# Half SwiGLUs with three pairs of places for split weights, splits queued one weight ahead, and normed operands after the third column block

## The chip, the cores and the metric

One core of a Trainium2 chip runs the whole program in one launch. The metric is device time in microseconds, the median of several executions. The profile is one more execution, recorded by the hardware profiler; its span goes from the first to the last instruction of the program. Engines: TensorE (PE for matmuls, PEld for its weight loads), VectorE (DVE), ScalarE (ACT), GpSimd (POOL) and SyncE (SP), which here only issues DMAs.

## What is computed

One step of a two-layer diffusion backbone on 128 context and 256 latent tokens, model width 1024, all in float32. Every sub-layer is an RMSNorm with a shift and a scale from the condition (adaLN), a mixer, and a gated residual. The two layers are

```
even: half SwiGLU -> gated DeltaNet | windowed attention -> half SwiGLU
odd : half SwiGLU -> bidirectional gated linear attention -> half SwiGLU
```

and the four half SwiGLUs, which the change is about, are each

```
h = rmsnorm(x) * (1 + scale) + shift
x = x + 0.5 * gate * ((silu(h @ Wg) * (h @ Wu)) @ Wd)      # Wg, Wu: 1024 x 2816, Wd: 2816 x 1024
```

Context and latent tokens have their own shift, scale and gate: nine vectors of 1024 a layer (18 in all, two streams each), each of them `silu(cond) @ ada_w + ada_b`.

## The kernel before

**Layout.** Activations lie transposed: 128 channels on the partitions, 8 blocks (`KD`) of channels, 384 tokens (`T`) in the free dimension. To keep float32 accuracy every matmul is done three times: weights and activations are split in a high and a low part in the `F32R` format, and `products` (L189) issues low x high, high x low and high x high for every block of 128 input channels.

**Splitting a weight.** `split_w` takes a 128 x 1024 tile `w` from a ring of three places, loads it with a DMA on SyncE's queue (L174), copies it on ScalarE to `wh` (L176) and lets VectorE subtract, `wl = w - wh` (L177). `wh` and `wl` come from a ring of two places each. A place comes free when the products that read it are done.

**A half SwiGLU** (`ffn`, called four times, f = 0 to 3) goes through four stages. In the first gate and up stage, called h1 below, it makes 11 column blocks j of 128: a product with the gate weight (24 matmuls), one with the up weight (24 more), `scaled` (L203: VectorE multiplies the PSUM result by `rb`, the reciprocal norm of each token), silu on ScalarE (L332), the multiplication (L337), and a split of the result into `ah` and `al` (L181, L182). In the first down stage, a1, eight output blocks m are made of two weights each, of 768 and 640 columns (18 and 15 matmuls, 33 an m), and added to x (`residual`, L305, two instructions, one per token stream). Then the same for the other 11 column blocks (h2) and the rest of the down projection (a2). In a2 the next norm is prepared behind each m: `norm_tile` (L247, L249) scales x to `hh` and `hl`, `square_tile` sums squares, and after the last m `end_norm` makes `rb` by way of two small matmuls (L289, L297) and a copy (L300).

**The norm is applied late.** `hh` and `hl` hold x times the scale, without the norm. The shift stands as two more columns (`TC` = 386), so that the product with the shift falls out of the same matmul and is added as a bias behind `scaled`.

**adaLN steps.** While a half SwiGLU runs, VectorE also works out later adaLN vectors: `ada_rows` loads 128 x 1024 tiles of `ada_w` (`aw`, two places, a DMA on SyncE's queue, L103), and multiplies each for both streams into accumulators (L145 for the first tile, L147 for the seven others). One such instruction is one step, 16 steps a vector; then `ada_sum` sums over partitions with 16 small matmuls (L161) and `ada_end` stores the vector. f = 0 makes five vectors, f = 1 and f = 2 four each, f = 3 one. The steps are put in by the local function `between`: two or three after each j, two after each m of a1, one after each m of a2, queued behind that block's last VectorE instruction. The order of the engines' queues is otherwise the compiler's: it places instructions in program order, and takes a later one first where the earlier has to wait in its own model.

**Early weights.** Behind the last column blocks of f = 0 and f = 2, `side` splits five weights of the mixer that follows into places the mixer uses later (`Even.weights`, `Odd.weights`).

## Time and profile before

| | |
|---|---|
| median of 3 runs | 1725.99 us (1721.74 to 1726.15) |
| the profiled execution | 1724.06 us; span 1722.3 us |
| PE busy | 1656.9 us, 96% of the span |
| DVE / ACT / POOL busy | 72% / 44% / 0% |
| mean granted TensorE clock | 0.985 |

The profile's page counts a pipelined matmul as busy from its start to a modelled end, and two matmuls overlap. A busy PE is therefore not yet a PE that could go no faster; what shows its pace is how many matmuls a stretch holds. DMA issues are not counted as busy.

### The profile page before, as it was taken

How to read it: one execution, taken by the hardware profiler on the slowest of the kernel's cores; microseconds unless marked ns; L12 is line 12 of the kernel's file. 1: busy time of each engine (PE TensorE's matmuls, PEld its weight loads, DVE VectorE, ACT ScalarE, POOL GpSimd, SP SyncE). 2: the span in 40 equal slices, each digit the busy share in tenths (PEclk: the TensorE clock that was granted, in tenths of full speed). 3: DMA queues.
4: the chain of work that ended last, by engine and by line, in shares of the span. 5: the costliest groups of instructions: out<-in, count | busy, mean ns of one | idle time of the engine just before them, and what ended most of it. 6: DMA issues, size and time to landing. Idle time of an engine off the chain costs nothing.

```text
span 1722.3 us, 26237 instructions
## 1 busy us (share of the span) xinstructions
PE 1656.9 (96%) x10341; PEld 1570.9 (91%) x10341; DVE 1237.5 (72%) x2091; ACT 749.2 (44%) x1301; POOL 0.2 (0%) x4
## 2 busy tenths in 40 slices
PE   5999998999999999999999999999999999999997
PEld 3998998899888899989999998999898889999997
DVE  3887787777868768877856887786567768744554
ACT  4432343366336443323344432344655754433343
POOL 0000000000000000000000000000000000000000
PEclk8999999999999989999999999999999999999998
DMA  8566666451321226666644656574313354434332
GB/s 321 183 186 186 204 205 210 148 188 62 114 78 50 77 84 196 180 198 196 185 132 147 197 187 198 188 228 135 102 62 96 102 172 147 159 111 136 126 110 95
DMA packets 80376, 261.83 MB, mean 152 GB/s; under 512 B 9691, under 2 KB 11739, under 8 KB 80124
## 3 DMA queue, kind: packets, MB, share of 16 engines
q1 hardware_dynamic: 80252, 260.15, 47.8%
q8 instruction: 81, 1.33, 0.3%
q14 instruction: 43, 0.35, 0.1%
HBM read 255.13 MB, written 4.98 MB: 151 GB/s over the span
## 4 chain that ended last, share of the span: by engine, by line
PE 82%; DVE 10%; DMA 4%; issue 2%; ACT 2%; SPq 0%; DVEq 0%; ACTq 0%
PE acc L189 71%; DVE acc L147 3%; DVE wl L177 2%; DMA aw<-in_adaw_dram 2%; PE ada L161 1%; DVE x L305 1%; DMA w<-in_evw_dram 1%; DMA w<-in_wdn_dram 1%; PE ps L679 1%; PE ps L683 1%; PE ada L113 1%; PE ss L289 1%; PE ps L1139 1%; PE ps L647 0%; DVE ssum L276 0%
## 5 line engine op out<-in xcount | busy, mean ns | idle before, releaser
L176 ACT CAST wh<-w 128x1024 fp32r<-128x1024 f32 (+1 forms) x358 | 340.2, 951 | 683.5 <-PE acc L189 491.0
L189 PE MATMUL acc<-hh,wl 128*128 128x386 f32 x1728 | 595.3, 345 | 7.3 <-DVE wl L177 7.2
L189 PE MATMUL acc<-hl,wh 128*128 128x386 f32 x1728 | 589.6, 341 | 0.0
L189 PE MATMUL acc<-hh,wh 128*128 128x386 f32 x1728 | 587.9, 340 | 0.0
L177 DVE TENSOR_TENSOR wl<-w,wh 128x1024 fp32r<-128x1024 f32 (+1 forms) x358 | 392.3, 1097 | 98.3 <-ACT wh L176 96.8
L189 PEld LDWEIGHTS acc<-hh,wl 128*128 128x128 f32 x1728 | 325.6, 188 | 19.4 <-DVE wl L177 9.5
L189 PEld LDWEIGHTS acc<-hl,wh 128*128 128x128 f32 x1728 | 327.2, 189 | 2.3 <-issue 0.8
L189 PEld LDWEIGHTS acc<-hh,wh 128*128 128x128 f32 x1728 | 325.5, 188 | 2.3 <-issue 0.8
L189 PE MATMUL acc<-ah,wl 128*128 128x384 f32 x704 | 242.2, 344 | 17.2 <-DVE wl L177 16.8
L147 DVE SCALAR_TENSOR_TENSOR acc<-aw,cs,acc 128x1024 f32<-128x1024 f32 x196 | 243.1, 1278 | 8.4 <-DMA aw<-in_adaw_dram 8.4
L189 PE MATMUL acc<-al,wh 128*128 128x384 f32 x704 | 238.5, 339 | 0.0
L189 PE MATMUL acc<-ah,wh 128*128 128x384 f32 x704 | 238.4, 339 | 0.0
L189 PEld LDWEIGHTS acc<-ah,wl 128*128 128x128 f32 x704 | 132.7, 189 | 27.9 <-DVE wl L177 27.9
L189 PEld LDWEIGHTS acc<-al,wh 128*128 128x128 f32 x704 | 132.9, 189 | 0.0
L189 PEld LDWEIGHTS acc<-ah,wh 128*128 128x128 f32 x704 | 132.8, 189 | 0.0
L203 DVE TENSOR_TENSOR tu<-acc,rb 128x386 f32<-128x386 f32 x88 | 49.2, 559 | 105.7 <-PE acc L189 105.6
L203 DVE TENSOR_TENSOR tg<-acc,rb 128x386 f32<-128x386 f32 x138 | 76.6, 555 | 55.3 <-PE acc L189 52.0
L305 DVE SCALAR_TENSOR_TENSOR x<-acc,hg,x 128x128 f32<-128x128 f32 (+1 forms) x128 | 47.5, 413 | 68.5 <-PE acc L189 68.5
L332 ACT ACTIVATE sg<-tg 128x128 f32<-128x128 f32 (+1 forms) x176 | 70.6, 448 | 51.6 <-DVE tg L203 51.5
L337 DVE SCALAR_TENSOR_TENSOR a<-tu,sg 128x128 f32<-128x128 f32 (+1 forms) x176 | 65.7, 415 | 8.3
L181 ACT CAST ah<-a 128x384 fp32r<-128x384 f32 x88 | 45.3, 515 | 41.5 <-DVE a L337 41.3
L182 DVE TENSOR_TENSOR al<-a,ah 128x384 fp32r<-128x384 f32 x88 | 48.6, 552 | 3.5 <-ACT ah L181 3.5
(368 smaller groups left out, 1502.4 us busy)
## 6 DMA issues: line engine op xcount, KB each, us to landing
w<-in_wgu_dram SPq DMA_DIRECT2D x176, 512.0 KB, 3.7
aw<-in_adaw_dram SPq DMA_DIRECT2D x144, 512.0 KB, 4.2
w<-in_wdn_dram SPq DMA_DIRECT2D x64, 384.0 KB, 3.1
w<-in_wdn_dram SPq DMA_DIRECT2D x64, 320.0 KB, 3.0
w<-in_evw_dram SPq DMA_DIRECT2D x24, 512.0 KB, 4.1
w<-in_odw_dram SPq DMA_DIRECT2D x24, 512.0 KB, 3.6
w<-in_evo_dram SPq DMA_DIRECT2D x8, 512.0 KB, 3.5
w<-in_odo_dram SPq DMA_DIRECT2D x8, 512.0 KB, 4.0
```

Of the source, the lines that this page charges most:

```text
L113: nc.tensor.matmul(ps[32 * g:32 * g + 32, 0:256], self.cs[:, k, :], w[:, 256 * g:256 * g + 256], start=k == 0, stop=k == KD - 1)
L147: nc.vector.scalar_tensor_tensor(t, w, cs, t, op0=ALU.mult, op1=ALU.add)
L161: self.nc.tensor.matmul(ps[32 * g:32 * g + 32, 0:256], self.pick[:, s], acc[s][:, 256 * g:256 * g + 256], start=s == 0, stop=s == 1)
L176: nc.scalar.copy(wh[:, 0:n], w[:, 0:n])
L177: nc.vector.tensor_tensor(wl[:, 0:n], w[:, 0:n], wh[:, 0:n].bitcast(F32), op=ALU.subtract)
L181: self.nc.scalar.copy(hi, src)
L182: return self.nc.vector.tensor_tensor(lo, src, hi.bitcast(F32), op=ALU.subtract)
L189: self.nc.tensor.matmul(out, s[:, sl], mv[:, k0 + k], start=first and k == 0 and i == 0, stop=last and k == nk - 1 and i == 2)
L203: self.nc.vector.tensor_tensor(t[0:m], p, self.rb[0:m], op=ALU.mult)
L305: i = nc.vector.scalar_tensor_tensor(self.x[:, k, lo:hi], p[:, lo:hi], gate[:, k, s:s + 1], self.x[:, k, lo:hi], op0=ALU.mult, op1=ALU.add)
L332: nc.scalar.activation(sg[:, lo:hi], tg[:, lo:hi], AF.Silu, bias=tg[:, T + s:T + s + 1])
L337: nc.vector.scalar_tensor_tensor(a32[:, lo:hi], tu[:, lo:hi], tu[:, T + s:T + s + 1], sg[:, lo:hi], op0=ALU.add, op1=ALU.mult)
```

## The change

1. `split_w` takes every third pair of weight places of a half SwiGLU from the pool of that half SwiGLU, so that three pairs rotate in place of two.
2. `ffn` lists its 76 weights in the order of use, and `weights(n)` splits the next one before it hands out the present one: in program order every split stands one weight ahead.
3. `between` goes. `n` steps for each weight fall due behind the split, queued behind its VectorE instruction (`issue_after(self.last_split.ins)`): 2.8 a column block in f = 0 and 2.4 in the others, none in the first three; one a weight in a1, half a one in a2.
4. The DMAs of `ada_rows` are issued on GpSimd's queue, and every third `aw` tile has a place of its own, three in all.
5. From the fourth column block on (`raw = 3`), the products read `nh` and `nl`: x with norm, scale and shift applied, split once. `normed` makes them, eight blocks k over the first three j. These products have 384 columns, silu reads PSUM and is one instruction, and `scaled` and the two multiplications become one multiplication from PSUM.
6. Three weights instead of five are split early for each mixer, and three places (`XT`, `BR`, `mhl`) move to the mixer's own pool. The late steps also sum a vector one step pair earlier.

```diff
@@ -98,9 +99,9 @@
-    def ada_tile(self, v, k, pool=None):
+    def ada_tile(self, v, k, pool=None, queue=None):
         w = (pool or self.adar).tile([128, 1024], F32, tag="aw", name=self.name("aw"))
-        self.nc.sync.dma_start(w, self.a["adaw"][v // 2, k, v % 2])
+        (queue or self.nc.sync).dma_start(w, self.a["adaw"][v // 2, k, v % 2])
         return w
@@ -136,16 +137,16 @@
         for v in vs:
-            acc = [pool.tile([128, 1024], F32, tag=f"acc{s}", bufs=2, name=self.name("acc")) for s in range(2)]
+            acc = [pool.tile([128, 1024], F32, tag="acc", bufs=4, name=self.name("acc")) for s in range(2)]
             for k in range(KD):
-                w = self.ada_tile(v, k)
+                w = self.ada_tile(v, k, pool if k % 3 == 2 else None, nc.gpsimd)
                 for s in range(2):
                     t, cs = acc[s], self.cs[:, k, s:s + 1]
                     if k == 0:
                         nc.vector.tensor_scalar(t, w, cs, None, op0=ALU.mult)
                     else:
                         nc.vector.scalar_tensor_tensor(t, w, cs, t, op0=ALU.mult, op1=ALU.add)
-                    if k == 1 and s == 1 and ready:
+                    if k == 0 and s == 1 and ready:
                         self.ada_sum(*ready)
@@ -170,16 +171,20 @@
         nc = self.nc
+        if self.third and not to:
+            self.turn += 1
+            if self.turn % 3 == 0:
+                to = [self.third.tile([128, 1024], F32R, tag=t, name=self.name(t)) for t in ("wh", "wl")]
         w = self.ring.tile([128, 1024], F32, tag="w", bufs=3, name=self.name("w"))
         nc.sync.dma_start(w[:, 0:n], src)
         wh, wl = to or [self.ring.tile([128, 1024], F32R, tag=t, bufs=2, name=self.name(t)) for t in ("wh", "wl")]
         nc.scalar.copy(wh[:, 0:n], w[:, 0:n])
-        nc.vector.tensor_tensor(wl[:, 0:n], w[:, 0:n], wh[:, 0:n].bitcast(F32), op=ALU.subtract)
+        self.last_split = nc.vector.tensor_tensor(wl[:, 0:n], w[:, 0:n], wh[:, 0:n].bitcast(F32), op=ALU.subtract)
         return wh, wl
-    def split(self, hi, lo, src):
+    def split(self, hi, lo, src, engine=None):
         self.nc.scalar.copy(hi, src)
-        return self.nc.vector.tensor_tensor(lo, src, hi.bitcast(F32), op=ALU.subtract)
+        return (engine or self.nc.vector).tensor_tensor(lo, src, hi.bitcast(F32), op=ALU.subtract)
@@ -189,12 +194,13 @@
-    def proj(self, src, m=128):
+    def proj(self, src, m=128, h=None):
         w = src if isinstance(src, tuple) else self.split_w(src, KD * m)
         p = self.acc.tile([128, 512], F32, tag="acc", name=self.name("acc"))
-        self.products(p[0:m, 0:TC], w, self.hh, self.hl, KD, m, True, True)
-        return p[0:m, 0:TC]
+        n = TC if h is None else T
+        self.products(p[0:m, 0:n], w, *(h or (self.hh, self.hl)), KD, m, True, True)
+        return p[0:m, 0:n]
@@ -307,39 +313,73 @@
         return i
-    def ffn(self, f, l, gate, after, rows=(), side=iter(()), skip=0):
+    def ffn(self, f, l, gate, after, rows=(), side=iter(()), skip=0, steps=2):
         nc = self.nc
+        gs, shift = self.gs, self.m(l, gate - 2)
         hg = self.small.tile([128, KD, 2], F32, tag="hg", name=self.name("hg"))
         with self.tc.tile_pool(name=self.name("ffn"), bufs=1) as pool:
             ah = pool.tile([128, NF // 2, T], F32R, name=self.name("ah"))
             al = pool.tile([128, NF // 2, T], F32R, name=self.name("al"))
-            work = lambda tag, n: pool.tile([128, n], F32, tag=tag, bufs=2, name=self.name(tag))
+            h = [pool.tile([128, KD, T], F32R, name=self.name(t)) for t in ("nh", "nl")]
             rows = self.ada_rows(rows, pool) if rows else iter(())
-            def between(last, n):
-                with self.tc.issue_after(last.ins):
-                    for _ in range(n):
-                        next(rows, None)
+            self.third = pool
+            raw, due = 3, 0.0
+            wgu, wdn = self.a["wgu"], self.a["wdn"]
+            srcs = []
+            for half in range(2):
+                srcs += [(wgu[f, i], 1024) for i in range(NF * half, NF * half + NF)]
+                srcs += [(wdn[f, half, m, :, c0:c1], (c1 - c0) * 128) for m in range(KD) for c0, c1 in ((0, 6), (6, 11))]
+            srcs.reverse()
+            ready = [self.split_w(*srcs.pop())]
+            def weights(n):
+                nonlocal due
+                if srcs:
+                    ready.append(self.split_w(*srcs.pop()))
+                    due += n
+                    with self.tc.issue_after(self.last_split.ins):
+                        while due >= 1:
+                            next(rows, None)
+                            due -= 1
+                return ready.pop(0)
+            def normed(k):
+                t = self.tmp.tile([128, T], F32, tag="xg", name=self.name("nx"))
+                nc.vector.tensor_tensor(t, self.x[:, k], self.rb[:, 0:T], op=ALU.mult)
+                for s, lo, hi in STREAMS:
+                    nc.scalar.activation(t[:, lo:hi], t[:, lo:hi], AF.Identity, bias=shift[:, k, s:s + 1],
+                                         scale=gs[:, k, s:s + 1])
+                self.split(h[0][:, k], h[1][:, k], t)
             for half in range(2):
                 for jj in range(NF // 2):
                     j = half * (NF // 2) + jj
-                    pg = self.proj(self.a["wgu"][f, 2 * j])
-                    tg = self.scaled(pg)
-                    sg = work("sg", T)
-                    for s, lo, hi in STREAMS:
-                        nc.scalar.activation(sg[:, lo:hi], tg[:, lo:hi], AF.Silu, bias=tg[:, T + s:T + s + 1])
-                    pu = self.proj(self.a["wgu"][f, 2 * j + 1])
-                    tu = self.scaled(pu, work("tu", TC))
-                    a32 = work("a32", T)
-                    for s, lo, hi in STREAMS:
-                        nc.vector.scalar_tensor_tensor(a32[:, lo:hi], tu[:, lo:hi], tu[:, T + s:T + s + 1],
-                                                       sg[:, lo:hi], op0=ALU.add, op1=ALU.mult)
-                    last = self.split(ah[:, jj], al[:, jj], a32)
+                    hj, n = (None, 0.0) if j < raw else (h, steps / 2)
+                    pg = self.proj(weights(n), h=hj)
+                    a = pool.tile([128, T], F32, tag="a", bufs=3, name=self.name("a"))
+                    if j < raw:
+                        tg = self.scaled(pg)
+                        for s, lo, hi in STREAMS:
+                            nc.scalar.activation(a[:, lo:hi], tg[:, lo:hi], AF.Silu, bias=tg[:, T + s:T + s + 1])
+                        for k in range(KD * j // raw, KD * (j + 1) // raw):
+                            normed(k)
+                    else:
+                        nc.scalar.activation(a, pg, AF.Silu)
+                    pu = self.proj(weights(n), h=hj)
+                    if j < raw:
+                        tu = self.scaled(pu)
+                        for s, lo, hi in STREAMS:
+                            nc.vector.scalar_tensor_tensor(a[:, lo:hi], tu[:, lo:hi], tu[:, T + s:T + s + 1],
+                                                           a[:, lo:hi], op0=ALU.add, op1=ALU.mult)
+                    else:
+                        nc.vector.tensor_tensor(a, pu, a, op=ALU.mult)
+                    self.split(ah[:, jj], al[:, jj], a)
                     if j >= skip:
                         next(side, None)
-                    between(last, 2 + j % 2)
                 if half == 0:
                     nc.vector.tensor_scalar(hg, self.m(l, gate), 0.5, None, op0=ALU.mult)
                 else:
@@ -347,15 +387,14 @@
                     for c0, c1 in ((0, 6), (6, 11)):
-                        w = self.split_w(self.a["wdn"][f, half, m, :, c0:c1], (c1 - c0) * 128)
-                        self.products(p[:, 0:T], w, ah, al, c1 - c0, 128, c0 == 0, c1 == 11, k0=c0)
-                    last = self.residual(p, m, hg)
-                    between(last, 2 - half)
+                        self.products(p[:, 0:T], weights(1.0 - half / 2), ah, al, c1 - c0, 128, c0 == 0, c1 == 11, k0=c0)
+                    self.residual(p, m, hg)
                     if half == 1:
                         next(side, None)
                         after(m)
             for _ in rows:
                 pass
+            self.third = None
@@ -385,7 +424,7 @@
         self.early = {}
-        for j, tag, bufs in ((0, "LA", 6), (1, "LA", 6), (2, "LA", 6), (8, "XT", 2), (9, "BR", 2)):
+        for j, tag, bufs in ((0, "LA", 6), (1, "LA", 6), (2, "LA", 6)):
             to = tuple(self.tl([128, 1024], tag, bufs, F32R) for _ in range(2))
...
-        XX = self.tl([128, 2, 4, 128], "XT", 2)
+        XX = self.t([128, 2, 4, 128], "XT", 2)
...
@@ -894,7 +933,7 @@
         self.early = {}
-        halves = [t[:, 1024 * i:1024 * i + 1024] for tag, k in (("Q", 2), ("S1", 2), ("vn", 3), ("mhl", 3))
+        halves = [t[:, 1024 * i:1024 * i + 1024] for tag, k in (("Q", 2), ("S1", 2), ("vn", 3))
                   for t in [self.tl([128, 1024 * k], tag, F32R)] for i in range(k)]
@@ -1177,12 +1216,12 @@
         even = Even(n, o, late, n.norm_after(0, 2, 6, 7))
-        n.ffn(0, 0, 2, n.norm_after(0, 1, 3, 4), (2, 3, 4, 5, 6), even.weights(), 18)
+        n.ffn(0, 0, 2, n.norm_after(0, 1, 3, 4), (2, 3, 4, 5, 6), even.weights(), 18, 2.8)
         even.run(n.ada(7))
-    n.ffn(1, 0, 8, n.norm_after(1, 0, 0, 1), (8, 9, 10, 11))
+    n.ffn(1, 0, 8, n.norm_after(1, 0, 0, 1), (8, 9, 10, 11), steps=2.4)
     with tc.tile_pool(name="odd_late", bufs=1) as late:
         odd = Odd(n, o, late, n.norm_after(1, 2, 6, 7))
-        n.ffn(2, 1, 2, n.norm_after(1, 1, 3, 4), (12, 13, 14, 15), odd.weights(), 18)
+        n.ffn(2, 1, 2, n.norm_after(1, 1, 3, 4), (12, 13, 14, 15), odd.weights(), 18, 2.4)
         odd.run(n.ada(16))
@@ -1192,7 +1231,7 @@
-    n.ffn(3, 1, 8, final, (17,))
+    n.ffn(3, 1, 8, final, (17,), steps=2.4)
     rb = n.end_norm(last=True)
```

## Rows read from the trace of the kernel before

**Rows 1.** The page, part 1: engine, busy us, share of the span, instructions.

```profile
PE 1656.9 (96%) x10341; PEld 1570.9 (91%) x10341; DVE 1237.5 (72%) x2091; ACT 749.2 (44%) x1301; POOL 0.2 (0%) x4
```

**Rows 2.** Stretches, L189 alone: from:to length, PE, PEld, clock, DMA: f=0's a2, f=3's h2, a2.

```profile
283.50:342.90 59.40, 49.83 (x266) 47.58 (x265) 0.94 0.48 152
1568.05:1661.20 93.15, 93.15 (x530) 93.15 (x529) 1.00 0.39 123
1661.20:1707.85 46.65, 46.65 (x266) 46.54 (x264) 1.00 0.33 95
```

**Rows 3.** Stretches, L189 alone: a1 of f = 0, and the sum over f = 0 to 2.

```profile
132.20:185.50 53.30, 48.33 (x266) 45.49 (x265) 1.00 0.64 193
...
sum 158.80, PE 145.37 PEld 136.86; mean PE 48.46 PEld 45.62
```

**Rows 4.** Stretches, L189 alone: h2 of f = 0, and the sum over f = 0 to 2.

```profile
185.50:283.50 98.00, 95.08 (x530) 92.58 (x529) 1.00 0.67 214
...
sum 292.70, PE 285.01 PEld 277.64; mean PE 95.00 PEld 92.55
```

**Rows 5.** Timeline of VectorE in a1 of f = 0: start, length, instruction, idle before it.

```profile
152.46 0.74 DVE L305 SCALAR_TENSOR_TENSOR x<-acc,hg,x 128x128 f32<-128x128 f32 x2 [1.89 <-PE acc L189]
153.12 1.27 DVE L147 SCALAR_TENSOR_TENSOR acc<-aw,cs,acc 128x1024 f32<-128x1024 f32 x1
...
154.98 0.82 DVE L177 TENSOR_TENSOR wl<-w,wh 128x640 fp32r<-128x640 f32 x1
...
158.94 0.74 DVE L305 SCALAR_TENSOR_TENSOR x<-acc,hg,x 128x128 f32<-128x128 f32 x2 [1.53 <-PE acc L189]
```

**Rows 6.** Groups by line, shapes apart: count | busy us, mean ns | idle before.

```profile
L177 DVE TENSOR_TENSOR wl<-w,wh 128x1024 fp32r<-128x1024 f32 x228 | 277.8, 1220 | 30.9 <-ACT wh L176 30.1
L147 DVE SCALAR_TENSOR_TENSOR acc<-aw,cs,acc 128x1024 f32<-128x1024 f32 x196 | 243.1, 1278 | 8.4 <-DMA aw<-in_adaw_dram 8.4
L177 DVE TENSOR_TENSOR wl<-w,wh 128x768 fp32r<-128x768 f32 x64 | 61.2, 957 | 66.0 <-ACT wh L176 65.7
L177 DVE TENSOR_TENSOR wl<-w,wh 128x640 fp32r<-128x640 f32 x64 | 52.6, 821 | 0.5
L182 DVE TENSOR_TENSOR al<-a,ah 128x384 fp32r<-128x384 f32 x88 | 48.6, 552 | 3.5 <-ACT ah L181 3.5
L176 ACT CAST wh<-w 128x1024 fp32r<-128x1024 f32 x228 | 239.5, 1051 | 429.3 <-PE acc L189 272.0 <-issue 138.5 <-ACT sg L332 11.9
```

**Rows 7.** Groups by line, shapes together, the same columns.

```profile
L305 DVE SCALAR_TENSOR_TENSOR x<-acc,hg,x 128x128 f32<-128x128 f32 (+1 forms) x128 | 47.5, 413 | 68.5 <-PE acc L189 68.5
L181 ACT CAST ah<-a 128x384 fp32r<-128x384 f32 x88 | 45.3, 515 | 41.5 <-DVE a L337 41.3
L247 ACT ACTIVATE hh<-x,gs 128x128 fp32r<-128x128 f32 x96 | 38.6, 447 | 15.1 <-DVE x L305 14.2 <-DVE gs L237 0.9
L161 PE MATMUL ada<-acc,pick 128*32 128x256 f32 x224 | 19.1, 387 | 0.5 <-DVE acc L147 0.4
```

**Rows 8.** The chain that ended last, in a2 of f = 0: start, length, what.

```profile
287.40 3.67 DVE acc L147 x3
```

**Rows 9.** Stretches, all engines: PE, PEld, DVE, ACT, POOL, clock, DMA.

```profile
292.20:299.00 6.80, 4.50 (x14) 4.50 (x15) 2.98 (x5) 0.48 (x2) 0.00 (x0) 0.50 0.67 221
365.00:435.00 70.00, 70.00 (x422) 67.84 (x421) 54.18 (x135) 47.55 (x95) 0.00 (x0) 0.98 0.21 68
930.70:949.60 18.90, 18.90 (x109) 18.74 (x107) 14.69 (x20) 9.21 (x14) 0.00 (x0) 1.00 0.51 166
1236.00:1262.00 26.00, 26.00 (x162) 26.00 (x161) 13.70 (x20) 17.81 (x34) 0.00 (x0) 0.97 0.00 1
```

**Rows 10.** Groups of VectorE from 930.7 to 949.6 us, columns as in rows 6.

```profile
L147 DVE SCALAR_TENSOR_TENSOR acc<-aw,cs,acc 128x1024 f32<-128x1024 f32 x3 | 3.7, 1278 | 0.0
...
L145 DVE TENSOR_SCALAR acc<-aw,cs 128x1024 f32<-128x1024 f32 x2 | 1.4, 750 | 0.0
```

**Rows 11.** DMA issues: count, size, median us to landing.

```profile
aw<-in_adaw_dram SPq DMA_DIRECT2D x144, 512.0 KB, 4.2
```

More of the change, by code (lines that the diff above doesn't have):

```diff
@@ L53, in __init__ @@
         self.made = set()
+        self.third, self.turn = None, 0
         self.setup()
@@ L662, in group @@
         four = lambda v: v.unsqueeze(1).to_broadcast([128, 4, 128])
-        XX = self.tl([128, 2, 4, 128], "XT", 2)
+        XX = self.t([128, 2, 4, 128], "XT", 2)
         X, XT = XX[:, 0], XX[:, 1]
-        BR = self.tl([128, 2, 4, 128], "BR", 2)
+        BR = self.t([128, 2, 4, 128], "BR", 2)
         B, R = BR[:, 0], BR[:, 1]
@@ L927, in operands @@
         if half == 0:
-            m = self.tl([128, 2, 4, T], "mhl", F32R)
+            m = self.t([128, 2, 4, T], "mhl", dt=F32R)
             self.mh, self.ml = [m[:, 0]], [m[:, 1]]
```

## The prediction

> **What bounds the kernel now.** I read the page's engine line first: PE counts as busy for 96% of the span [rows 1]. That figure hides the losses, because overlapping matmuls with modelled ends fill short gaps, so I measured pace by the number of matmuls in a stretch. In f = 3, which has one adaLN vector and is done with it early, h2 takes 93.15 us for its 528 matmuls and a2 takes 46.65 us for 264 (the counts in the rows take in two neighbours): 176.4 and 176.7 ns a matmul, at full clock and with nothing in between [rows 2]. The chain of waits names PE alone there. That is the floor of a stage; what the other half SwiGLUs take above it is what this change can reach.
>
> The three a1 stages with adaLN steps take 158.80 us together [rows 3], 18.85 above 3 x 46.65. The three h2 stages take 292.70 [rows 4], 13.25 above 3 x 93.15. The a2 of f = 0 takes 59.40 [rows 2], 12.75 above. The h1 stages hold the end of the norm before; I count no gain there.
>
> The timeline shows why a1 loses. At 152.46 PE has finished a block m; the place of its 640-column weight comes free, and ScalarE starts the copy for the next one. VectorE does the residual, then two adaLN steps, and only at 154.98 the subtraction, which ends at 155.80 [rows 5]. PE meanwhile has the 18 matmuls of the 768-column weight, 18 x 0.1767 = 3.18 us, and is through at 155.64. With two long steps of 1.28 us instead of one long and one short, VectorE is half a microsecond later still. The period is 158.94 - 152.46 = 6.48 us where 33 matmuls need 5.83. VectorE is not short of time: two subtractions 0.957 + 0.821, the residual 2 x 0.413, two steps 2 x 1.278 are 5.16 us a block [rows 6, 7]. What is missing is a free place early enough, and the steps stand before the subtraction that PE waits for.
>
> In a2 of f = 0 the same happens at once and larger: three steps stand in a row for 3.67 us [rows 8] ahead of a residual and of two subtractions, PE runs dry, and from 292.2 to 299.0 the granted clock is 0.50, the 1.2 GHz level, with 14 matmuls [rows 9].
>
> **Part 1: three pairs, splits ahead, steps behind them.** The place of a weight is now free two weights before its use, and each step is queued behind the split of the next weight. In a1 VectorE's 5.16 us fit into 5.83, so PE should never wait; a1 falls to its floor and the inherent sum. A sum's 16 matmuls are 19.1 / 14 = 1.4 us [rows 7]; by the count of steps one falls into each a1 before and after. Gain: 18.85 - 3 x 1.4 = 14.65 us. In h2 there are two sums each (in f = 1 and f = 2 one may slip to a2, at the same price): 13.25 - 6 x 1.4 = 4.85 us. In a2 of f = 0 VectorE has a block's two subtractions 1.78, residual 0.83, one step 1.28, the norm's two scaled differences (as the residual's, 0.83) and the sum of squares (as L182, 0.55): 5.27 of 5.83. The step order and the fifth early weight, which made the long stall, are gone, and with the stall the stretch at half clock. I take 12.5 of the 12.75. Together 32.0 us; nothing, if VectorE's queue stays in the old order.
>
> **Part 2: normed operands.** From the fourth block on a column block costs VectorE two subtractions, one multiplication from PSUM (as L182), one split and 2.8 steps: 2 x 1.22 + 2 x 0.55 + 2.8 x 1.28 = 7.1 us [rows 6] under 48 matmuls of 8.47. So the higher rate of steps is covered. That PE saves two columns of 386 I cost at nothing: the rows with 386 and with 384 columns have the same pace, 176.4 and 176.7 ns [rows 2].
>
> The Trainium skill, "TensorE: Matmul & The Clock Gate", section "Back-to-back issue gap", gives an isolated gap of N/2.4 + 2.5 ns; by it 2 columns of 3648 matmuls (48 x 19 x 4) would be 0.83 ns each, an estimate of 3.0 us more gain and a time of 1698. The same section says that in a stream the weight load sets the spacing too, and the rows side with that.
>
> What normed operands cost is the start. In the first three blocks `normed` adds, for eight k, a multiplication and a subtraction on VectorE (2 x 0.552) and two scalings and a copy on ScalarE (2 x 0.447 + 0.515) [rows 6, 7]: 8.8 and 11.3 us. In f = 0 the norm is made before the first two adaLN vectors, and this has three whole blocks, 25 us. In f = 1 to 3 `rb` comes only after the stage has begun; in f = 2 from that copy at 930.7 to the fourth block at 949.6 there are 18.9 us, in which VectorE is busy 14.69 and ScalarE 9.21 [rows 9]. The steps there (3.7 + 1.4) go away [rows 10]. VectorE then has 14.69 - 5.1 + 8.8 = 18.4 of 18.9, ScalarE 9.21 + 11.3 = 20.5. The last k is read 21 matmuls into the block, 3.7 us later, so 22.6 us are there for the last k, but the weight for that block must be split by 949.6. Lower bound no wait. Upper bounds: one k after the other, 8 x 2.51 = 20.1 us with VectorE's other 9.6 in line, 29.7 against 22.6, is 7.1 us late; with ScalarE's 9.2 in line too, 16.3. ScalarE alone is over by 1.6, which is the nearest row; with hand-overs I take 2.0, three times: 6.0 us.
>
> **Part 3: adaLN loads on GpSimd's queue, three places.** This takes 112 loads out of SyncE's queue, in which a load that waits for its place holds up the weight load behind it. POOL has no other work [rows 1]. A tile feeds two steps; at 2.8 steps a block it is used every 2/2.8 x 8.47 = 6.05 us, so with three places a load may take 3 x 6.05 - 2.56 = 15.6 us before VectorE waits; on SyncE's queue it takes 4.2 [rows 11]. Cost nothing; a tile that is later than that holds VectorE's whole queue, the splits too.
>
> **Part 4: two early weights fewer for each mixer.** Each is then split inside the mixer: 1.05 us ScalarE and 1.22 VectorE [rows 6], 4.5 us for two if nothing hides them, 0 if all is hidden. In the even mixer, before these weights are used, VectorE is busy 54.18 of 70 us and PE all of it; in the odd one 13.70 of 26 [rows 9]. Room is there, more in the odd one: I take 1.5 and 0.5.
>
> **Part 5: the tail of f = 0.** Due steps are 22.4 + 16 + 30.8 + 7 or so, 76 of the 82; six remain, four of them VectorE instructions where one remained before. The 3.8 us stand behind the norm's end while the even mixer starts. 0 to 3.8; I take 0.5.
>
> **Sum.** 32.0 - 6.0 - 1.5 - 0.5 - 0.5 = 23.5 us. The profiled execution took 1724.06 us (span 1722.3); it lies 1.9 below the median of the runs, within their spread. 1724.06 - 23.5 = 1700.6: I say 1701.
>
> **Rivals.** (a) All cover holds and the start of f = 1 to 3 costs nothing: 1724.06 - 32 = 1692. For it: the third pair lets splits be done ahead. Against: ScalarE's 20.5 in 18.9. Chance 0.12. (b) The start runs k after k, 7.1 us late in three half SwiGLUs: 1724.06 - 32 + 21.3 + 2.5 = 1716. For it: two engines hand each k to and fro in queues that go in order. Chance 0.15. (c) The change doesn't do what it says in the down stages: the compiler had already taken one subtraction ahead of the residual, and if steps still stand before the wanted one, a1's 14.65 are not had: 1724.06 - 32 + 14.65 + 8.5 = 1715. Against: the steps are tied behind the split. Chance 0.1. (d) The other side: the start of f = 1 to 3 goes fully one after the other, 16.3 us late each: 1724.06 - 32 + 48.9 + 2.5 = 1743. It decides from (32 - 2.5) / 3 = 9.8 us late each. Against: most of this work has no order between k. Chance 0.05. (e) GpSimd's issues and VectorE hold each other up, one VectorE instruction of 1.28 us a load: an a1 block then needs 5.16 + 1.28 = 6.44 us against 5.83, 0.6 x 24 = 14.6 us in all; a column block with steps 7.1 + 1.4 x 1.28 = 8.9 against 8.47, 0.43 x 57 = 24.5; together 39 over the forecast, 1740. It decides from about 1.1 us a load on. Against: nothing in the trace, where POOL is idle [rows 1]; for it: nothing either. Chance 0.03.
>
> The Trainium skill, "SBUF — State Buffer", sections "SBUF: two separate sides" and "Who interferes with whom", is what makes me list (e): it has VectorE and GpSimd share one pair of SBUF ports, taken for a whole instruction by whichever comes first, and has a DMA issued from GpSimd depend on that pair. No run here shows it so far.
>
> The forecast has the remaining 0.55. A difference under 0.3%, 5.2 us, is about what a measurement of this kernel can't tell from no change, so faster means under 1720.8. (a), the forecast and most of (b) and (c) are there: 0.88; same 0.05, where (b) and (c) meet; slower 0.07. The range takes in the forecast, (b) and (c) and most of (a): 1690 to 1718.
>
> **What the profile after would show.** Right: a1 of f = 0 to 2 at 48 us each, with wl ahead of the steps in the timeline; a2 of f = 0 at 47 and no stretch at 0.50 in it; the idle time of PE behind wl near zero; waits in f = 1 to 3 at the start of the fourth block, for `nh`, `nl` or wl, of 1 to 3 us. Wrong: such a wait over 5 us, VectorE idle behind aw, or the mixers longer by more than 3 us each.

## The result, and the profile after

The changed kernel takes 1693.43 us (median of 4 runs, 1693.03 to 1694.66) against 1724.07 for the kernel before in the same sessions: ratio 0.9824, 95% interval 0.9806 to 0.9841, a gain of 30.6 us. The profiled execution took 1694.66 us, span 1692.9, which is 29.4 us less span than before. The forecast was 1701.

The page's engine line of the changed kernel, as [rows 1]:

```profile
PE 1641.2 (97%) x10341; PEld 1572.8 (93%) x10341; DVE 1183.4 (70%) x1927; ACT 753.5 (45%) x1321; POOL 59.7 (4%) x116
```

PE's share barely moves, as it did not show the losses either. What PE waited for does show them. The view of waits, PE alone, kernel before and then changed kernel (total us, times, longest):

```profile
PE acc L189 <- DVE wl L177: 24.0, 27, 4.9
```

```profile
PE acc L194 <- DVE wl L182: 5.0, 2, 2.7
...
PE ss L295 <- ACT sq L280: 3.4, 2, 2.1
PE ps L686 <- DVE X L691: 2.8, 1, 2.8
```

Of 27 waits for wl two are left; a second wait for `sq` (the kernel before has one, of 1.3 us) and one for `X` are new and come up below. Stretches of the changed kernel's matmul line, L194, as [rows 2 to 4]: a1 of f = 0 and the sum over f = 0 to 2, h2 the same, a2 of f = 0, a2 of f = 1, h2 of f = 3.

```profile
130.73:178.44 47.71, 46.78 (x266) 46.19 (x265) 1.00 0.67 213
...
sum 143.31, PE 140.52 PEld 138.74; mean PE 46.84 PEld 46.25
...
178.44:274.52 96.08, 93.45 (x530) 92.23 (x529) 1.00 0.70 219
...
sum 284.26, PE 279.77 PEld 277.35; mean PE 93.26 PEld 92.45
...
274.52:322.11 47.59, 46.54 (x266) 46.22 (x265) 1.00 0.52 165
847.95:899.88 51.93, 47.05 (x266) 46.20 (x265) 0.99 0.49 150
...
1538.80:1631.44 92.64, 92.64 (x529) 92.64 (x529) 1.00 0.39 120
```

a1 falls from 158.80 to 143.31 us, h2 from 292.70 to 284.26, a2 of f = 0 from 59.40 to 47.59, with no stretch at 0.50 in it. The a2 of f = 1 is longer, 51.93 where it took 46.78, and so is the a2 of f = 2, 47.9 against 46.8: in f = 1 and f = 2 one of the two sums of adaLN vectors that stood in h2 now stands in a2 (by the places of the sums' matmuls, L162).

VectorE in a1 of f = 0 of the changed kernel, the place of [rows 5]:

```profile
149.18 0.96 DVE L182 TENSOR_TENSOR wl<-w,wh 128x768 fp32r<-128x768 f32 x1
150.06 1.28 DVE L148 SCALAR_TENSOR_TENSOR acc<-aw,cs,acc 128x1024 f32<-128x1024 f32 x1
152.26 0.82 DVE L182 TENSOR_TENSOR wl<-w,wh 128x640 fp32r<-128x640 f32 x1 [0.92 <-ACT wh L181]
153.00 1.28 DVE L148 SCALAR_TENSOR_TENSOR acc<-aw,cs,acc 128x1024 f32<-128x1024 f32 x1
154.20 0.73 DVE L311 SCALAR_TENSOR_TENSOR x<-acc,hg,x 128x128 f32<-128x128 f32 x2
154.97 0.96 DVE L182 TENSOR_TENSOR wl<-w,wh 128x768 fp32r<-128x768 f32 x1
```

Each wl now stands ahead of a step, and the period is 154.97 - 149.18 = 5.79 us, the 33 matmuls alone, where it was 6.48.

The start of the normed operands, which was to cost 2.0 us in each of f = 1 to 3, costs next to nothing. The view of the tile `nl`, who waited for it in the whole program:

```profile
L187 DVE TENSOR_TENSOR nl<-nx,nh x32: 547/552/559, 36.8 to 1426.9; 128x384 fp32r<-128x384 f32 x32
...
  PEld acc L194: 0.4, 1
```

That wait is in f = 3, where the eighth and last `nl` is done just as it is read. From the timelines of ScalarE, PE and VectorE: the copy of `rb`, the first matmul of the fourth block, the last `nl`, and the matmul that reads it:

```profile
1406.08 0.48 ACT L306 COPY rb<-rb 128x384 f32<-128x384 f32 x1 [3.45 <-PE rb L303]
...
1423.15 0.34 PE L194 MATMUL acc<-nh,wl 128*128 128x384 f32 x1
...
1426.89 0.55 DVE L187 TENSOR_TENSOR nl<-nx,nh 128x384 fp32r<-128x384 f32 x1
...
1427.50 0.44 PE L194 MATMUL acc<-nl,wh 128*128 128x384 f32 x1
```

In f = 1 the last `nl` is done 0.4 us before it is read, in f = 2 2.6 us.

What is new is at the end of f = 1's a2. Timelines of PE, ScalarE and VectorE there, and the stretch behind it over all engines:

```profile
895.59 0.34 PE L194 MATMUL acc<-ah,wh 128*128 128x384 f32 x1
895.76 0.28 PE L295 MATMUL ss<-ones,ssum 128*128 128x1 f32 x2
898.18 0.38 PE L295 MATMUL ss<-ones,sq 128*128 128x1 f32 x2 [2.14 <-ACT sq L280]
...
899.88 0.67 PE L194 MATMUL acc<-hh,wl 128*128 128x386 f32 x1
```

```profile
895.96 1.04 ACT L181 CAST wh<-w 128x1024 fp32r<-128x1024 f32 x1 [1.56 <-PE acc L194]
```

```profile
897.04 1.23 DVE L182 TENSOR_TENSOR wl<-w,wh 128x1024 fp32r<-128x1024 f32 x1 [0.33 <-ACT wh L181]
```

```profile
898.70:905.50 6.80, 6.80 (x25) 6.80 (x25) 2.95 (x11) 1.84 (x3) 0.00 (x0) 0.50 0.65 227
```

The copy of the first weight of f = 2 starts only when a2's last product is done, so its wl is ready at 898.27; and the small matmuls of the norm (L295), which wait for the last `sq`, stand ahead of the first products. PE has only those small matmuls for 899.88 - 895.59 = 4.3 us, and the granted clock then is 0.50, the 1.2 GHz level, for 6.8 us. The reason of the late copy is the count: a half SwiGLU has 76 weights, `turn` runs on, and the first weight of f = 2 is number 2 x 76 + 1 = 153 = 3 x 51, so it takes the third pair, in the pool that f = 1 is still using.

### The profile page after: what moved, and what is told of

It reads as the page before. It is cut to its first block, busy times and chain, and to the rows that moved or that the text cites. A ratio compares the mean times of both kernels' runs of the same rounds, so it can differ in the third digit from the quotient of the medians.

```text
span 1692.9 us, 26114 instructions
## 1 busy us (share of the span) xinstructions
PE 1641.2 (97%) x10341; PEld 1572.8 (93%) x10341; DVE 1183.4 (70%) x1927; ACT 753.5 (45%) x1321; POOL 59.7 (4%) x116
## 4 chain that ended last, share of the span: by engine, by line
PE 90%; DVE 4%; DMA 3%; ACT 2%; issue 1%; SPq 0%; DVEq 0%; ACTq 0%
PE acc L194 79%; DMA aw<-in_adaw_dram 2%; PE ada L162 1%; PE ps L1178 1%; PE ps L722 1%; DVE wl L182 1%; ACT wh L181 1%; DMA w<-in_wgu_dram 1%; PE ps L718 1%; PE ada L114 1%; PE ss L295 0%; PE ps L686 0%; DMA w<-in_evw_dram 0%; PE ps L759 0%; DMA x<-in_x_dram 0%
## 5 line engine op out<-in xcount | busy, mean ns | idle before, releaser
L181 ACT CAST wh<-w 128x1024 fp32r<-128x1024 f32 (+2 forms) x362 | 343.4, 949 | 543.5 <-PE acc L194 295.7
L182 DVE TENSOR_TENSOR wl<-w,wh 128x1024 fp32r<-128x1024 f32 (+2 forms) x362 | 398.5, 1101 | 237.6 <-ACT wh L181 234.6
L194 PE MATMUL acc<-nh,wl 128*128 128x384 f32 x1216 | 410.6, 338 | 0.0
L194 PE MATMUL acc<-nh,wh 128*128 128x384 f32 x1216 | 410.1, 337 | 0.0
L194 PE MATMUL acc<-nl,wh 128*128 128x384 f32 x1216 | 409.7, 337 | 0.1
L148 DVE SCALAR_TENSOR_TENSOR acc<-aw,cs,acc 128x1024 f32<-128x1024 f32 x196 | 248.5, 1279 | 13.0 <-DMA aw<-in_adaw_dram 13.0
L194 PE MATMUL acc<-ah,wl 128*128 128x384 f32 x704 | 238.2, 338 | 0.0
L194 PE MATMUL acc<-ah,wh 128*128 128x384 f32 x704 | 237.7, 338 | 0.0
L194 PE MATMUL acc<-al,wh 128*128 128x384 f32 x704 | 237.2, 337 | 0.0
L194 PEld LDWEIGHTS acc<-nh,wl 128*128 128x128 f32 x1216 | 228.2, 188 | 3.5 <-issue 1.6
L194 PEld LDWEIGHTS acc<-nl,wh 128*128 128x128 f32 x1216 | 228.3, 188 | 0.4 <-DVE nl L187 0.4
L194 PEld LDWEIGHTS acc<-nh,wh 128*128 128x128 f32 x1216 | 228.2, 188 | 0.0
L194 PE MATMUL acc<-hh,wl 128*128 128x386 f32 (+2 forms) x544 | 191.9, 353 | 5.1 <-DVE wl L182 5.0
L194 PE MATMUL acc<-hl,wh 128*128 128x386 f32 (+2 forms) x544 | 190.9, 351 | 0.0
L194 PE MATMUL acc<-hh,wh 128*128 128x386 f32 (+2 forms) x544 | 189.5, 349 | 0.0
L194 PEld LDWEIGHTS acc<-ah,wl 128*128 128x128 f32 x704 | 132.1, 188 | 2.1 <-issue 2.1
L194 PEld LDWEIGHTS acc<-al,wh 128*128 128x128 f32 x704 | 132.1, 188 | 0.0
L194 PEld LDWEIGHTS acc<-ah,wh 128*128 128x128 f32 x704 | 132.1, 188 | 0.0
L194 PEld LDWEIGHTS acc<-hh,wl 128*128 128x128 f32 (+2 forms) x544 | 104.4, 192 | 7.7 <-DVE wl L182 3.3
L194 PEld LDWEIGHTS acc<-hl,wh 128*128 128x128 f32 (+2 forms) x544 | 104.7, 192 | 1.5
```

The source lines that it names most:

```text
L148: nc.vector.scalar_tensor_tensor(t, w, cs, t, op0=ALU.mult, op1=ALU.add)
L181: nc.scalar.copy(wh[:, 0:n], w[:, 0:n])
L182: self.last_split = nc.vector.tensor_tensor(wl[:, 0:n], w[:, 0:n], wh[:, 0:n].bitcast(F32), op=ALU.subtract)
L194: self.nc.tensor.matmul(out, s[:, sl], mv[:, k0 + k], start=first and k == 0 and i == 0, stop=last and k == nk - 1 and i == 2)
```

## The experiments

Each ran beside the kernel before on one chip. The stage lengths in this table run from the first matmul of a stage to the first of the next, in each kernel's profiled execution (us). Beside the experiments the kernel before took 1721.19, 1720.91 and 1722.71 us in its three sessions, so that small differences between rows are read by the ratios:

| kernel | median | a1, f = 0-2 | h2, f = 0-2 | a2 f = 0 | a2 f = 1 | even mixer | odd mixer | span |
|---|---|---|---|---|---|---|---|---|
| before | 1724.07 | 158.8 | 292.7 | 59.4 | 46.8 | 282.7 | 208.5 | 1722.3 |
| changed | 1693.43 | 143.3 | 284.3 | 47.6 | 51.9 | 283.2 | 208.2 | 1692.9 |
| two pairs | 1702.60 | 144.5 | 284.2 | 50.7 | 47.8 | 285.1 | 206.2 | 1702.0 |
| steps behind the block | 1701.83 | 144.4 | 286.5 | 51.2 | 51.9 | 284.2 | 208.3 | 1700.4 |
| both of these | 1735.87 | 166.3 | 289.1 | 54.3 | 49.2 | 285.5 | 208.2 | 1737.7 |
| third pair alone | 1687.89 | 142.6 | 289.2 | 47.3 | 46.3 | 280.1 | 206.9 | 1686.1 |
| splits not ahead | 1693.45 | 143.3 | 283.7 | 47.6 | 51.4 | 284.2 | 208.6 | 1692.6 |
| no normed operands | 1697.58 | 143.2 | 285.2 | 47.5 | 52.3 | 283.8 | 208.9 | 1697.0 |
| 386 columns | 1700.86 | 143.6 | 286.3 | 47.7 | 51.4 | 282.6 | 209.6 | 1698.5 |
| loads on SyncE | 1693.48 | 143.3 | 283.5 | 47.6 | 51.4 | 287.6 | 209.3 | 1692.9 |
| count set back | 1690.40 | 143.2 | 283.5 | 47.6 | 48.0 | 285.1 | 209.2 | 1691.4 |
| third pair, three early | 1693.95 | 142.6 | 289.0 | 47.3 | 46.3 | 286.7 | 206.6 | 1693.0 |
| no early weight | 1700.50 | 143.3 | 283.7 | 47.6 | 52.3 | 292.1 | 208.7 | 1699.7 |
| normed in f = 1, 3 | 1684.47 | 143.3 | 284.7 | 47.5 | 48.0 | 278.8 | 210.2 | 1685.9 |

**Place or order?** First each undone alone, then both.

```diff
-            self.third = pool
+            self.third = None
```

> The changed kernel, but with two pairs of places for split weights as before; order, steps, normed operands and GpSimd loads stay. If the place is what ended the waits (P), the a1 stages of f = 0 to 2 go back from 47.6 to about 52.5 us and the a2 of f = 0 to 53 or more: 1709 to 1720 us. If the order of VectorE's queue is what ended them (O), a1 stays at 48, since a split that starts when the place comes free still has one whole weight of PE time, 2.6 us or more, for 0.83 + 0.96 us of work. Apart from both: in the changed kernel's trace every third weight, the one in the third pair, runs at 173.3 ns a matmul and the two others at 176.8; if that goes with the pair, its loss costs 2112 x 3.5 ns = 7.4 us. O then gives 1701, P 1716 to 1727.

```diff
-                    with self.tc.issue_after(self.last_split.ins):
-                        while due >= 1:
-                            next(rows, None)
-                            due -= 1
...
-                    self.split(ah[:, jj], al[:, jj], a)
+                    last = self.split(ah[:, jj], al[:, jj], a)
...
+                    between(last)
...
-                    self.residual(p, m, hg)
+                    between(self.residual(p, m, hg))
```

> The changed kernel, but the adaLN steps that fall due are queued where they were before: behind a block's last VectorE instruction (the split of the product, or the residual), not behind the split of the next weight. Three pairs and splits one weight ahead stay. P (the place): the split has two weights of lead, the steps in front of it do no harm, a1 at 48, 1693 to 1696. O (the order): a1 of f = 0 to 2 back to about 52.5 and the a2 of f = 0 longer too: 1708 to 1720.

`between` here holds the four removed lines and queues the due steps behind the instruction that it is given, the last of VectorE in the block. Both kernels lose 8 to 9 us (ratios to before 0.9885, 0.9852 to 0.9918, and 0.9882, 0.9856 to 0.9908), and a1 stays at 144.5 in both. The first alone would speak for the order (O expected this a1 and 1701 us), the second for the place (P expected this a1, but 1693 to 1696 us). So the two were undone together.

> The changed kernel with both undone: two pairs of places, and the steps queued behind a block's last VectorE instruction. Splits one weight ahead, normed operands and GpSimd loads stay. Each undoing alone left the a1 stages of f = 0 to 2 at 47.5 to 48.9 us. If place and order each suffice (either), undoing both brings the old queue back, a step or two in front of a subtraction that can't start early: a1 at 52 to 53 in f = 0 to 2, a2 of f = 0 at 54 or more, 1715 to 1727. If it was the splits one ahead, the third aw place or VectorE's lower load (other), a1 stays at 48: 1700 to 1708.

1735.87 us, ratio 1.0087 (1.0072 to 1.0102): slower than before, and 9 us above the expected range. Its a1 stages are 7.5 us longer than in the kernel before; what makes them longer stays open. VectorE in a1 of f = 0, with three pairs and the steps behind the block, and then with two pairs and the same order:

```profile
150.06 0.74 DVE L311 SCALAR_TENSOR_TENSOR x<-acc,hg,x 128x128 f32<-128x128 f32 x2 [1.04 <-PE acc L194]
150.72 2.47 DVE L148 SCALAR_TENSOR_TENSOR acc<-aw,cs,acc 128x1024 f32<-128x1024 f32 x2
153.11 1.72 DVE L182 TENSOR_TENSOR wl<-w,wh 128x768 fp32r<-128x768 f32 x2
155.84 0.74 DVE L311 SCALAR_TENSOR_TENSOR x<-acc,hg,x 128x128 f32<-128x128 f32 x2 [1.02 <-PE acc L194]
```

```profile
152.43 0.74 DVE L311 SCALAR_TENSOR_TENSOR x<-acc,hg,x 128x128 f32<-128x128 f32 x2 [1.88 <-PE acc L194]
153.09 2.47 DVE L148 SCALAR_TENSOR_TENSOR acc<-aw,cs,acc 128x1024 f32<-128x1024 f32 x2
155.48 0.82 DVE L182 TENSOR_TENSOR wl<-w,wh 128x640 fp32r<-128x640 f32 x1
...
159.26 0.74 DVE L311 SCALAR_TENSOR_TENSOR x<-acc,hg,x 128x128 f32<-128x128 f32 x2 [1.83 <-PE acc L194]
```

In both, two steps stand in front of the subtractions. With three pairs the period is 5.78 us all the same: both wl that follow are for weights whose turn is still to come. With two pairs it is 6.83. Place and order are two cures for one wait, and in the changed kernel either is enough; the order alone, in the kernel before, was not run. What each loses alone lies elsewhere: the h1 stages of f = 1 to 3 take 303.3 us with two pairs (295.3 in the changed kernel), h2 is 2.2 us longer with the steps behind the block, and a2 of f = 0 is longer by 3.1 and 3.6 us. There all the norm's small matmuls (L295) stand ahead of the mixer's first products, and PE runs small matmuls alone for 5.1 us with two pairs and 4.5 with the steps behind; in the changed kernel, where ten of these twelve matmuls come behind the first products, it is 1.4.

**The place alone.** The kernel before, with the new lines of `split_w` and the count set back for each half SwiGLU:

```diff
+            self.third, self.turn = pool, 0
```

> The kernel before with one thing more: every third pair of weight places of a half SwiGLU comes from its own pool. Steps stay where between put them, splits stand at their use, aw loads on SyncE with two places, no normed operands, five early weights. Either: a1 of f = 0 to 2 falls from 53 to 48, h2 by 1 to 2 us each, a2 of f = 0 from 59 to 48 to 53: 1700 to 1706 for a kernel before at 1721 to 1724. Other: a1 stays at 52 to 53, 1717 to 1722.

1687.89 us, ratio 0.9803 (0.9789 to 0.9818), 12 us below the expected range and 5.5 below the change in the median, with the old order of steps, no normed operands and five early weights. Its interval overlaps that of the change (0.9806 to 0.9841), but not that of the changed kernel with loads on SyncE (0.9825 to 0.9854), which takes as long as the change and was measured beside it. Its a1, f = 0 and sum:

```profile
132.45:180.01 47.56, 46.63 (x265) 46.04 (x265) 1.00 0.67 214
...
sum 142.59, PE 139.80 PEld 138.04; mean PE 46.60 PEld 46.01
```

**Splits ahead.** `ready` starts empty, so that each split is written at its use.

```diff
-            ready = [self.split_w(*srcs.pop())]
+            ready = []
```

> The changed kernel with each split written at its use, not one weight ahead; three pairs of places and the steps behind the splits stay. Theory: the place decides, and writing the split ahead adds nothing to it: 1693 us, half SwiGLU stages a1 at 48. Rival, as the prediction took it: the split must stand ahead, or PE waits for wl at each weight once there are steps: a1 at 50 or more, 1705 us or above.

1693.45 us: no difference. With three pairs a split that is written at its use comes early enough; with two pairs this was not run.

**Normed operands and their width.** All products of h with `hh` and `hl`, without `nh`, `nl` and `normed`, at the same rate of steps; then normed operands with two idle columns more, which two copies fill, and products over `TC` columns.

```diff
-            raw, due = 3, 0.0
+            raw, due = NF, 0.0
...
```

> The changed kernel without normed operands: all 22 column blocks read hh and hl with 386 columns, and scaled, two silus and two multiplications come back in each; the plan of steps is kept. V (VectorE's load is what ended the waits): a column block with 2.8 steps needs 2.44 + 2.50 + 0.55 + 3.58 = 9.1 us of VectorE against 8.47 of PE in f = 0 and 8.6 in f = 1 and 2, so h1 and h2 of f = 0 grow by some 8 and 7 us, those of f = 1 and 2 by 1 to 2, and lateness is carried into a1: 1710 or more. O and P: waits in h of f = 0 only, as far as VectorE is over, and the first three blocks lose nothing: 1697 to 1708. If 386 columns cost what they differ by, 0.83 ns each in 3648 matmuls, 3 us of that.

```diff
-            h = [pool.tile([128, KD, T], F32R, name=self.name(t)) for t in ("nh", "nl")]
+            h = [pool.tile([128, KD, TC], F32R, name=self.name(t)) for t in ("nh", "nl")]
...
```

> The changed kernel with normed operands two columns wider: nh and nl get two columns more, filled with the shift's split and multiplied along but not used, so the 3648 matmuls behind the third block have 386 columns again; all else stays. By the pace of the kernel before, the same with 386 and with 384 columns, nothing changes: 1693. By 0.83 ns a matmul it is 3.0 us more: 1696. In the profile h2 of f = 3 tells it: 92.6 us or 93.1.

In the median it is 4.2 us slower without them (0.9856, 0.9831 to 0.988, which overlaps the change's interval) and 7.4 with 386 columns (0.9884, 0.9868 to 0.9901, which doesn't); the expectation for 386 columns was 3.0 at most. In the profiled executions 4.6 of the 5.6 us that 386 columns cost lie in the h stages. So the normed operands gain by their columns: with 386 columns VectorE is relieved as much, and nothing is gained. h2 of f = 3, which waits for nothing, takes 92.64 us at 384 columns and 93.2 to 93.6 at 386.

**The third pair's turn.**

```diff
-            self.third = pool
+            self.third, self.turn = pool, 0
```

> The changed kernel, with the count that picks every third weight set to 0 at the start of each half SwiGLU. In the changed kernel the first weight of f = 2 is number 153 = 3 x 51 and so gets the third pair, which lies in a pool opened anew over places that a2 of f = 1 still reads: it is split only after a2's last matmul, the norm's small matmuls stand before its products, and PE waits 4.3 us and then runs 6.8 us at a granted clock of 0.50. If that is the cause, the gap at the end of f = 1 goes to under 1 us and the stretch at half clock with it: 4.1 + 2.2 = 6 us less, 1687 to 1688. If the norm's end is late for another reason (ScalarE's square), the gap stays and the time is 1693.

a2 of f = 1 in this kernel:

```profile
850.87:898.86 47.99, 47.06 (x266) 46.19 (x265) 1.00 0.52 152
```

The wait is gone, and with it the stretch at half clock behind it. The whole gains 3.0 us (1690.40; 0.9818, 0.9795 to 0.9841), half of what was expected; the two intervals overlap, so the gain is seen in the stage and only likely in the total.

**GpSimd's queue.**

```diff
-                w = self.ada_tile(v, k, pool if k % 3 == 2 else None, nc.gpsimd)
+                w = self.ada_tile(v, k, pool if k % 3 == 2 else None)
```

> The changed kernel with the aw loads of the half SwiGLUs issued on SyncE's queue again, three places as in the changed kernel. If GpSimd's queue only moves the issue, since each load waits for a place that is free long before, the time stays at 1692 to 1695. If SyncE's queue is held up by an aw load that waits for its place and a weight load behind it comes late, PE waits for wl behind a weight DMA in a1 and in the h stages, some 0.5 us each time: 1697 to 1705.

1693.48 us: no difference in the total. In the profiled executions two differences cancel: h1 of f = 1 to 3 takes 291.2 us where it took 295.3, and the even mixer is 4.4 us longer, with the granted clock at 0.50 from 378.3 for 6.8 us, where the view of waits has no wait of PE ahead of it. Whether the queue has a part in either is not shown.

**Early weights.** The third pair alone once more, with three early weights for each mixer and `XT`, `BR`, `mhl` in the mixer's pool; and the changed kernel with none.

```diff
-        for j, tag, bufs in ((0, "LA", 6), (1, "LA", 6), (2, "LA", 6), (8, "XT", 2), (9, "BR", 2)):
+        for j, tag, bufs in ((0, "LA", 6), (1, "LA", 6), (2, "LA", 6)):
```

> The third pair alone on the kernel before gave 1687.9 us. Here it has, as in the change, three early weights for each mixer in place of five and four, so that two and one more are split inside the mixer. Theory: these weights are what makes the mixers longer in the changed kernel (even 283.2 against 280.1 us, odd 208.2 against 206.9, output products included); then even 283 and odd 208, 1692 us. Rival: the loss there comes from something else in the change (steps of f = 0 left for the start of the mixer, the operands' places); then 280 and 207, 1688 us.

> The changed kernel with no early weight at all, so that three more for each mixer are split inside it. Theory: by 1.5 us a weight in the even mixer (3.1 us for two there, from the third pair alone) and 1.3 a weight in the odd one, 8 us more: 1702 us. Rival: the mixers hide splits, and what was lost there had another cause: 1693 to 1695 us.

(The odd mixer had five too, not four.) Two weights fewer cost 6.1 us in the median (1693.95; 0.9833, 0.9814 to 0.9852, an interval that touches that of the third pair alone), all of it in the even mixer, 6.6 in the profile; the odd mixer is 0.4 shorter. PE in the even mixer, at the first step of the solve, first with five early weights and then with three; and the stretch behind it with three, all engines:

```profile
413.77 0.64 PE L114 MATMUL ada<-aw,cs 128*32 128x256 f32 x8
415.28 0.44 PE L194 MATMUL acc<-hh,wl 128*128 128x386 f32 x1 [0.87 <-DVE wl L182]
```

```profile
415.38 1.06 PE L114 MATMUL ada<-aw,cs 128*32 128x256 f32 x14
419.25 0.62 PE L654 MATMUL ps<-X,mh 128*128 128x24 f32 x2 [2.80 <-DVE X L659]
```

```profile
419.10:425.90 6.80, 6.58 (x24) 6.46 (x24) 3.67 (x8) 0.53 (x1) 0.00 (x0) 0.50 0.61 221
```

With five, products of a projection fill the wait for VectorE; with three they are not there, PE waits 2.8 us for `X`, and the clock is at 0.50 for 6.8 us. The changed kernel has the same wait (2.8 us, in the view of waits above). Of the 6.6 us this is 1.0 up to the matmul that waits and 3.9 behind it. The other 1.7 lie ahead of the solve, in a part with half the clock from 381.5 for 3.4 us and no wait of PE, and are not shown to come of the weights. From the matmul that waits to the end of the even mixer all kernels here with three early weights take 189.6 to 191.4 us, those with five 186.8 to 187.2. With no early weight the even mixer takes 292.1 us and the whole 1700.50 (0.9875, 0.9855 to 0.9895), 7.1 more than the change with three, 1.5 us below the expectation.

**A version from these.** The changed kernel with the count set back, normed operands only in f = 1 and f = 3, and five early weights:

```diff
-            raw, due = 3, 0.0
+            raw, due = 3 if f % 2 else NF, 0.0
```

> The changed kernel with the count of turns set back to 0 at the start of each SwiGLU, with normed operands only in f = 1 and 3, behind which no mixer comes, and with five and four early weights as before. Theory: it has the mixers of the kernel with the third pair alone (even 280, odd 207 us) and, in f = 1 and 3, the h stages at 384 columns (about 1 us less each in four stages): 1685 us. Rival: the width gives nothing in so few stages, or the early weights cost as much in f = 0 and f = 2 as they save: 1688 to 1691 us.

1684.47 us (1683.05 to 1687.66), ratio 0.978 (0.9763 to 0.9797): faster than both kernels, by 9 us than the change. From the third pair alone (0.9803) its interval doesn't part it.

## Why the prediction was right, and where not

The direction, the place and the range were right; the sum was 6 us short (a gain of 23.5 forecast, 29.4 between the profiled executions), by terms that were mis-sized in both directions. The measured time stands beside that of rival (a), 1692, but not by its sum: a1, h2 and a2 of f = 0 gave 35.7 in place of 32, and 6.2 were lost in the a2 of f = 1 and f = 2. That the two meet is luck.

*Part 1, 32.0 us.* By the profiled stages a1 gave 15.5 (forecast 14.65), h2 8.4 (4.85; the third pair alone gives 3.5 of it, 2.3 are the two sums that moved to the a2 of f = 1 and f = 2, which grew by 1.2, with the count set back, and 1.1, and the rest holds the columns, 3 x 0.51 by h2 of f = 3, which had no wait to lose) and a2 of f = 0 11.8 (12.5). The size was right. The reason given was too wide: it took pair, splits ahead and order as one. The pair alone does it in a1 and in a2 of f = 0, writing splits ahead adds nothing to three pairs, and the order is a second cure for the same wait. The sentence "nothing, if VectorE's queue stays in the old order" is wrong, and so is the price of rival (c): with steps still in front of the subtraction and three pairs, a1 took 144.4. It was the step from "VectorE's 5.16 us fit into 5.83" that carried: where the work fits into the period, as here, its order inside the period needs one more place and nothing else.

*Part 2, start, -6.0 us.* The step that failed most. PE waited 0.4 us for `nl`, once in the program, and h1 of f = 1 to 3 together is 1.7 us longer than before, as long as without normed operands (295.3 and 295.6). The bound put all the work of ScalarE behind `rb` in front of the fourth block (20.5 in 18.9), but the last k may be 3.7 us later, which the same paragraph said, and 20.5 fits in the 22.6. From the copy of `rb` to the last `nl` it took 23.4, 22.4 and 21.4 us in f = 1, 2 and 3. The hand-overs, for which 2.0 was taken three times, cost 0.4 once, as VectorE and ScalarE worked on different k. Of the rivals (a) was right on this point, but by little: the 2.6 us to spare in f = 2 come of the norm's small matmuls that stand ahead of its first products, so that 21.1 us of its blocks are left behind the copy of `rb`; with the count set back these matmuls stand behind the first products, 18.9 us are left, and 0.2 are to spare.

*Part 2, width, 0.* Wrong. At 386 against 384 columns 7.4 us, against no normed operands 4.2; from h2 of f = 3, (93.15 - 92.64) / 528 = 0.97 ns a matmul, times 3648 is 3.5 us. The rows with both widths, on which 0 rested, were both of two pairs, and for h2 of f = 3 that holds: with two pairs it takes 93.35 us at 384 columns too. With three pairs it gains. The Trainium skill, "TensorE: Matmul & The Clock Gate", section "Back-to-back issue gap", has a formula for an isolated matmul by which two columns make 0.83 ns, an estimate of 3.0 us. The 0.97 ns of h2 of f = 3 agree with it in size, with three pairs and not with two; the two paces of one width, below, it doesn't tell of.

*Part 3, 0.* Right in the total: 1693.48 on SyncE's queue against 1693.43. Rival (e) has nothing for it: a GpSimd issue takes 531 ns by the profile's page, 112 of them, and a step of VectorE takes 1279 ns on the mean, where it was 1278 [rows 6]. VectorE was idle 13.0 us behind `aw` in all (9.9 with three places on SyncE's queue, 8.4 before [rows 6]), which the prediction had as a sign of being wrong; a1 and h2, 143.3 and 283.5 us with the loads on SyncE, show no cost of it. The port that the Trainium skill, "SBUF — State Buffer", section "Who interferes with whom", has the two engines share shows in no row here.

*Part 4, -2.0.* Net, the even mixer is 0.5 us longer and the odd one 0.3 shorter. But with the third pair and five early weights the even mixer is shorter than before by 2.6 to 3.9 us, and against that two weights fewer cost 4.4 (changed against normed in f = 1, 3) to 5.0 us (third pair, three early against five, from the solve on), not 1.5. "Room is there" was read from the mean over 70 us; what decided was one place in which PE has nothing else in its queue.

*Part 5, -0.5.* Nothing: no step of f = 0 runs behind its a2, where in the kernel before one did.

*Not in the sum.* The a2 of f = 1, 5.1 us longer, 1.2 of it the sum that moved and 3.9 the wait at its end: the prediction never asked whose place the third pair takes at the start of a half SwiGLU.

*The profile after* met a1 at 48, a2 of f = 0 at 47.6 without half clock and nearly no wait for wl, and not the waits of 1 to 3 us at the fourth block.

Open: why the count set back gains only 3.0 us in total when its stage gains 3.9 and the clock behind it recovers. In its profile the even mixer is 1.9 us longer, 1.6 of them ahead of the solve, where a stretch at half clock stands that the changed kernel hasn't got, with no wait of PE ahead of it:

```profile
379.60:383.00 3.40, 3.40 (x15) 3.32 (x15) 1.84 (x11) 2.89 (x5) 0.00 (x0) 0.50 0.00 0
```

The same stretch is there with the loads on SyncE and with three early weights; what brings it is not known. Open too: the 8 us in h1 of f = 1 to 3 with two pairs, of which the view of waits shows 1.3, 1.8 and 1.8 beside a wait of 2.3 at the start of f = 1 that the other kernels have as well.

## What to carry to other kernels

Before reordering a queue, ask whether the buffer that the late work fills has one place too few: if all engines' work fits into the period, one more place makes the order inside it nearly free. When a rotation goes through a pool that opens and closes, count which turn falls on the first use after it opens. Work moved into a stage that looks half empty on average can meet the one place where PE has nothing else queued: two splits of 1.2 us cost 4 to 5 there, the half-clock stretch behind them included.

## What of the hardware was not expected

PE's pace without any wait goes in steps from weight to weight. h2 of f = 3 in the changed kernel, the first matmul of three weights that follow each other:

```profile
1538.80 0.33 PE L194 MATMUL acc<-nh,wl 128*128 128x384 f32 x1
...
1542.96 0.34 PE L194 MATMUL acc<-nh,wl 128*128 128x384 f32 x1
...
1547.20 0.34 PE L194 MATMUL acc<-nh,wl 128*128 128x384 f32 x1
```

24 matmuls take 4.16 us, then 4.24: 173.3 and 176.7 ns a matmul, and so on, one weight in three at the faster pace. At 386 columns every weight behind the first of h2 of f = 3 is at 176.2 to 177.5, with two or three pairs; at 384, in the changed kernel with two pairs, h2 of f = 3 runs at 176.7 behind its first weight, but a1 of f = 3 wholly at 173.3. So the fast pace is not simply a matter of the place of the weight, and what sets it stays open.

Short waits of PE cost more than themselves. Behind idle times of 2 to 3 us the granted clock was at 0.50 for 6.8 us at 898.7 and at 414.0 in the changed kernel, and at 419.1 with the third pair and three early weights; behind the same waits it was so for 3.4 us at 900.7 with splits not ahead and at 418.8 with 386 columns. At 898.7 it costs about 1.5 us on top of the 4 us of the wait, an estimate from two runs: h1 of f = 2 takes 97.5 us behind it, and 96.1 with the count set back. A wait is not the only thing that such a stretch stands behind: the one at 379.6, above, has none ahead of it.
